# A two-layer encoder on one core: where a group's background steps stand, and GpSimd's block copies in program order

## The chip, the core and the metric

The kernel runs on one core of a Trainium2 chip. The core has five engines that each work through a queue of their own in order, and wait for each other by semaphores: TensorE (PE, matrix multiplies), VectorE (DVE), ScalarE (ACT), GpSimd (POOL) and SyncE (SP, whose queue issues all DMA transfers here). The metric is the device time of one execution in microseconds (us), as the median of several runs; beside it one execution was recorded by the hardware profiler, and all rows quoted below come from that.

## The reference, cut to what matters

Two layers on 256 tokens of width 2048, all in float32. Each layer first makes q, k and v for two attentions and two gates from one projection of the normalised input; q and k are normalised per head before they are used:

```python
h = rmsnorm(x, norm_mix[l]) * (1.0 + sc_a) + sh_a
qa, ka, va, qb, kb, vb, ga, gb = split_cols(h @ w_in[l])
qa = rotary_partial(rmsnorm(qa.reshape(B, S, HA, HEAD_DIM), qn_a[l]), pos)
ka = rotary_partial(rmsnorm(ka.reshape(B, S, GA, HEAD_DIM), kn_a[l]), pos)
ya = window_attention(qa, ka, va, sink_a[l]) @ w_proj_a[l]
qb = rmsnorm(qb.reshape(B, S, HB, HEAD_DIM), qn_b[l])
kb = rmsnorm(kb.reshape(B, S, HB, HEAD_DIM), kn_b[l])
yb = neighbourhood_attention(qb, kb, vb, rel_bias_b[l]) @ w_proj_b[l]
merged = jax.nn.sigmoid(ga) * ya + jax.nn.sigmoid(gb) * yb
x = x + gt_a * (merged @ w_out[l])
```

A gated feed-forward network with a convolution over three tokens follows. The first attention has 8 query heads on 2 key heads (window of 128 tokens to each side), the second 8 heads on a 4 x 64 grid with a bias table.

## The kernel before

**Weights and halves.** All weights pass through the core once, in units of 16 blocks of 128 x 128 (1 MB). A unit is one transfer into a `raw` buffer (4 of them, shared with the rows of `ada_w`). Each unit has two halves; ACT casts a half to a rounded value (L348), and DVE subtracts that from the original (L349), so that every matrix product is made of high and low parts and comes out near float32. A half is the tile `hl`, of which there are 4 buffers: ACT can cast a half as soon as PE is done with the one four places earlier. On PE a product of tokens is the lines L464 to L466, a product of features L391, L392 or L395 to L397.

**Groups.** The q, k and v columns come in nine groups of 512 columns (`QKV_GROUPS`), group 0 being k and v of the first attention, groups 1 and 2 its q, and 3 to 8 the parts of the second (4 and 7 are v). A group is four units, so eight halves. In layer 2 (`l == 1`) a group is one pass: `tokens` makes its products, and then `qk_rows` does the normalisation in these steps:

- the squares on ACT (L651, sums in `qss`), a scaling and addition on DVE (L534), and the power -1/2 on POOL (L535, written to `qrs`);
- `norm`, some ticks later: DVE multiplies the sums in PSUM by `qrs` (L661) into `qn`, a tile with one buffer (`bufs=1`), and applies the rotation (L678 to L680). In layer 2 L661 is kept in program order on DVE's queue;
- `turn`, a tick after that: the rows become columns. Either PE transposes them (L697) and ACT scales the result (L698), or, for the groups in `MOVED_QK` (0, 1, 2 and 8 of layer 2), DVE transposes blocks of 32 x 32 (L685), POOL carries the blocks to their places with 16 copies (`moved_blocks`, L320), and three ticks later ACT scales them (L689).

**Attention as background.** The heads are a generator (`attention`, heads 0 to 7 of the first attention and then those of the second). A step of a head has scores on PE (L727), a mask and maximum on DVE (L730), exponentials and a division on ACT (L739, L747). In layer 2 the probabilities are then turned the same way, DVE's block transposition (L326) into the place of the head's q and the one before it, and 16 copies on POOL (L320, named `p<-spare` for head 0 and `p<-packA` or `p<-packB` for the others). After these come a split (L481, L484), the product with v (L766) and another split (L769, L770). DVE's other background work is the product of rows of `ada_w` with the condition (L248, named `aw`).

**Ticks.** Whatever is background runs at a tick, which comes once a unit, at its last block: first the functions that were deferred to this tick (`bg.defer`, `later`), then as many steps of the attention as its rate allows (0.4 a tick at first in layer 2), then the transfers of `ada_w` that a plan prescribes. A group ends with a unit, so one tick falls on the end of each group, and before the change it ran inside `tokens`, ahead of the group's squares and power.

**Order.** The instructions are recorded in the order in which the program emits them; a scheduler then sets each engine's queue and may move an instruction ahead of others, save for those that are wrapped in `tc.keep_in_program_order`, which keep their place among each other and the rest of the program's order on that engine.

Of the kernel before, what the change touches and what calls it, by code (L numbers as in the profile page):

```python
# [139 lines left out]
UB = 16  # L140
# [5 lines left out]
def encoder(ctx: ExitStack, tc: tile.TileContext, a: dict, out: bass.AP):  # L146
    nc = tc.nc
# [159 lines left out]
    bg = Paced()  # L307

    def later(n, fn):

        if n == 0:
            fn()
        else:
            bg.defer(lambda: later(n - 1, fn))

    def moved_blocks(dst, src):

        for b in range(0, P, BLOCK):
            for a in range(0, P, BLOCK):
                nc.gpsimd.tensor_copy(  # L320
                    out=dst[a : a + BLOCK, :, :, b : b + BLOCK], in_=src[b : b + BLOCK, :, :, a : a + BLOCK]
                )

    def turned_blocks(src, rows, n):

# [47 lines left out]
    class Wide:  # L373
# [9 lines left out]
        def turned(self):  # L383

            return [half.rearrange("p r q -> p q r") for half in self.halves]
# [13 lines left out]
    class Stream:  # L399
# [51 lines left out]
                    sums = [turned_back(p) for p in sums]  # L451
                evac(ps[:, : S + 2] if isinstance(acts[0], tuple) else sums if wide else sums[0])

        def tokens(self, h, kcs):

            pss = [mm.tile([P, 512], F32, name=f"ps{self.l}_{self.u}_t{t}", tag="mm") for t in range(2)]
            for kc in kcs:
                for _ in range(4):
                    hl, j = self.next_block()
                j -= 3  # L460
                hi, lo = (turns(hl[:, i, j * P : (j + 4) * P]) for i in range(2))
                for t, ps in enumerate(pss):
                    xh, xl = (h[kc][:, i, t * P : (t + 1) * P] for i in range(2))
                    nc.tensor.matmul(ps[:], xh, hi, start=kc == kcs[0], stop=False)  # L464
                    nc.tensor.matmul(ps[:], xh, lo, start=False, stop=False)  # L465
                    nc.tensor.matmul(ps[:], xl, hi, start=False, stop=kc == kcs[-1])  # L466
                if self.l == 0 and self.u == 1 and self.at == 4:
                    warm(WARM_ROW)
                if self.at == UB:
                    self.tick()  # L470
            return [turned_back(ps[:]) for ps in pss]

# [171 lines left out]
    def qk_rows(pss, heads, rot, gain, dst, then, moved=False, pinned=False):  # L644

        n = heads * HEAD
        ss = sm.tile([P, 8], F32, name="qss", tag="qss")
        for t, ps in enumerate(pss):
            for i in range(heads):
                sq = at.tile([P, HEAD], F32, name="qsq", tag="qsq", bufs=1)  # L650
                nc.scalar.activation(  # L651
                    out=sq[:], in_=ps[:, i // 2, i % 2 * HEAD : i % 2 * HEAD + HEAD], func=AF.Square,
                    accum_out=ss[:, t * heads + i : t * heads + i + 1],
                )
        rs = sm.tile([P, 8], F32, name="qrs", tag="qrs")
        rsqrt(rs[:, : 2 * heads], ss[:, : 2 * heads], HEAD, 2 * heads)
        def norm():
            qn = at.tile([P, 8 * HEAD], F32, name="qn", tag="qn", bufs=1)[:, : 2 * n]
            qn = qn.rearrange("p (t h d) -> p t h d", t=2, d=HEAD)
            for t, ps in enumerate(pss):  # L660
                product = nc.vector.tensor_tensor(  # L661
                    out=qn[:, t].rearrange("p (a h) d -> p a h d", h=2),
                    in0=ps[:, : heads // 2].rearrange("p a (h d) -> p a h d", d=HEAD),
                    in1=rs[:, t * heads : (t + 1) * heads].rearrange("p (a h) -> p a h", h=2).unsqueeze(3).broadcast_to([P, heads // 2, 2, HEAD]),
                    op=ALU.mult,
                )
                if pinned:
                    tc.keep_in_program_order(product)
            if rot is not None:
                x1, x2 = qn[:, :, :, :HALF], qn[:, :, :, HALF:ROT]  # L670
                tab = [rot[:, i].unsqueeze(2).broadcast_to([P, 2, heads, HALF]) for i in range(4)]
                tm = []
                for i in range(2):
                    z = ev.tile([P, S], F32, name=f"rt{i}", tag="z")
                    z = z[:].rearrange("p (i t h d) -> p i t h d", i=2, t=2, h=4)
                    tm += [z[:, 0, :, :heads], z[:, 1, :, :heads]]
                for i, src in enumerate((x1, x2, x2, x1)):
                    nc.vector.tensor_tensor(out=tm[i], in0=src, in1=tab[i], op=ALU.mult)  # L678
                nc.vector.tensor_tensor(out=x1, in0=tm[0], in1=tm[1], op=ALU.subtract)
                nc.vector.tensor_tensor(out=x2, in0=tm[2], in1=tm[3], op=ALU.add)  # L680
            bg.defer(lambda: turn(qn))

        def turn(qn):
            if moved:
                nc.vector.transpose(out=qn, in_=qn)  # L685
                moved_blocks(dst.rearrange("p h (t s) -> p h t s", t=2), qn.rearrange("p t h d -> p h t d"))

                def scaled():
                    tc.keep_in_program_order(nc.scalar.activation(out=dst, in_=dst, func=AF.Identity, scale=gain))  # L689
                    then()  # L690

                later(QK_STEPS, scaled)
                return
            for t in range(2):
                ps = ax.tile([P, 4, P], F32, name="qtp", tag="ax")
                for h in range(heads):
                    nc.tensor.transpose(ps[:, h], qn[:, t, h], ident[:])  # L697
                scaled = nc.scalar.activation(  # L698
                    out=dst[:, :, t * P : (t + 1) * P], in_=ps[:, :heads], func=AF.Identity, scale=gain
                )  # L700
                if pinned:
                    tc.keep_in_program_order(scaled)
            then()

        bg.defer(lambda: bg.defer(lambda: bg.defer(norm)))

    def in_halves(src, name, tag, yes):

# [183 lines left out]
    for l in range(L):  # L892
        st = Stream(l) if l == 0 else nxt
# [116 lines left out]
        for pi, (groups, gates) in enumerate(parts):  # L1010
            last = pi == len(parts) - 1
            for g, part in enumerate(groups):
                have_h(part)
                pss = st.tokens(h, part)
                if pi == max(0, len(parts) - 2) and g == 0:
                    gains, sink, cw, rots = small(l)
                dst = packs[g // 3][:, 4 * (g % 3) : 4 * (g % 3) + 4]
                rows = dst.rearrange("p (t a) s -> p t a s", t=2)
                if not last or pi > 0:
                    for t, ps in enumerate(pss):  # L1020
                        if pi == 0:
                            nc.scalar.copy(rows[:, t], ps)
                        else:
                            nc.vector.tensor_tensor(out=rows[:, t], in0=ps, in1=rows[:, t], op=ALU.add)
                    pss = [rows[:, t] for t in range(2)]
                if not last:
                    continue

                def turned(g=g):
                    ready[0] = g + 1  # L1030

                vcol = {0: 1, 4: 0, 7: 0}.get(g)
                if vcol is not None and pi == 0:
                    for t in range(2):
                        nc.scalar.copy(rows[:, t, vcol:], pss[t][:, vcol:])
                if g == 0:
                    qk_rows(pss, GA, rots[1], gains[:, 1:2], kTa, turned, g in MOVED_QK[l], l == 1)
                elif g < 3:
                    qk_rows(pss, 4, rots[0], gains[:, 0:1], dst, turned, g in MOVED_QK[l], l == 1)
                elif vcol is None:  # L1040
                    qk_rows(pss, 4, None, gains[:, 3:4] if g in (3, 6) else gains[:, 2:3], dst, turned, g in MOVED_QK[l], l == 1)
                else:
                    turned()
                if g == (1 if l in EARLY else 2):
                    bg.add(job, ATT[l])


            have_h(gates)
            for mo in range(BARE[0] if l else 0, KC):

                def gate_a(ps):
                    src, to = ps, pair(ya[:, mo])
                    if pi > 0:
                        nc.vector.tensor_tensor(out=to, in0=ps, in1=to, op=ALU.add)
                        src = to
                    if last:
                        half_tanh(to, src)
                    elif pi == 0:
                        nc.scalar.copy(to, ps)

                st.features([hs[k] for k in gates], [gate_a])
# [234 lines left out]
```

## Time and profile before

| | us |
|---|---|
| median of 3 runs | 2586.07 |
| lowest and highest run | 2584.91 and 2586.75 |
| the profiled execution | 2584.3 |
| its span, first to last instruction | 2581.7 |
| TensorE busy | 2547.9 (99%) |
| VectorE busy | 2212.6 (86%) |
| ScalarE busy | 1454.8 (56%) |
| GpSimd busy | 263.1 (10%), nearly all of it between 1376 and 1711 us |

The profile has tables (busy time by engine, by group of instructions, by stretch of time) and rows in order of time. A row gives its start in us from the span's beginning, its duration, the engine, the line, the operation, the tiles written and read, and the shape; in square brackets, where the engine was idle before it, how long, and what released it. The groups 0 to 8 of layer 2 are multiplied from about 1352 to 1562 us, and the first attention's heads run from about 1446 to 1590 us.

### The profile page before, as it was taken

How to read it: one execution, taken by the hardware profiler on the slowest of the kernel's cores; microseconds unless marked ns; L12 is line 12 of the kernel's file. 1: busy time of each engine (PE TensorE's matmuls, PEld its weight loads, DVE VectorE, ACT ScalarE, POOL GpSimd, SP SyncE). 2: the span in 40 equal slices, each digit the busy share in tenths (PEclk: the TensorE clock that was granted, in tenths of full speed). 3: DMA queues.
4: the chain of work that ended last, by engine and by line, in shares of the span. 5: the costliest groups of instructions: out<-in, count | busy, mean ns of one | idle time of the engine just before them, and what ended most of it. 6: DMA issues, size and time to landing. Idle time of an engine off the chain costs nothing.

```text
span 2581.7 us, 43544 instructions
## 1 busy us (share of the span) xinstructions
PE 2547.9 (99%) x17324; PEld 2378.3 (92%) x17324; DVE 2212.6 (86%) x3227; ACT 1454.8 (56%) x2432; POOL 263.1 (10%) x345
## 2 busy tenths in 40 slices
PE   8999999999999999999999999999999999999999
PEld 7999899999999999999998879999999999999998
DVE  8998998998998899799987778879889987766775
ACT  5445765456663665466565566654576546644663
POOL 0001100000000000000003668730000000000000
PEclk9999999999999999999999999999999999999999
DMA  9998789986778778777767667778848775555554
GB/s 370 352 349 306 263 299 356 335 315 227 259 292 307 258 285 297 291 279 279 281 226 271 262 229 264 258 284 332 309 175 294 291 295 197 206 201 197 204 202 147
DMA packets 102158, 699.97 MB, mean 271 GB/s; under 512 B 12866, under 2 KB 15170, under 8 KB 18114
## 3 DMA queue, kind: packets, MB, share of 16 engines
q1 hardware_dynamic: 101954, 697.20, 73.0%
q8 instruction: 135, 2.21, 0.3%
q14 instruction: 69, 0.56, 0.1%
HBM read 695.06 MB, written 2.10 MB: 270 GB/s over the span
## 4 chain that ended last, share of the span: by engine, by line
PE 70%; DVE 14%; DMA 6%; ACT 4%; issue 4%; POOL 2%; SPq 0%; ACTq 0%; DVEq 0%; POOLq 0%
PE ps L391 31%; PE ps L392 15%; DVE hl L349 5%; PE ps L397 5%; PE ps L395 5%; PE ps L396 5%; DVE aw L248 4%; DMA aw<-in_aw 3%; PE ps_t L465 2%; PE ps_t L464 2%; PE ps_t L466 2%; ACT hl L348 2%; DMA w<-in_ws 2%; POOL p L320 1%; DVE x L1108 1%
## 5 line engine op out<-in xcount | busy, mean ns | idle before, releaser
L349 DVE TENSOR_TENSOR hl<-w,hl 128x1024 fp32r<-128x1024 f32 x928 | 1130.3, 1224 | 215.4 <-ACT hl L348 213.1
L348 ACT CAST hl<-w 128x1024 fp32r<-128x1024 f32 x928 | 964.7, 1046 | 587.0 <-PE ps L392 253.8
L391 PE MATMUL ps<-h,hl 128*128 128x512 f32 x2432 | 796.8, 382 | 0.0
L392 PE MATMUL ps<-h,hl 128*128 128x256 f32 x2432 | 662.9, 273 | 0.0
L391 PEld LDWEIGHTS ps<-h,hl 128*128 128x128 f32 x2432 | 459.7, 189 | 64.0
L392 PEld LDWEIGHTS ps<-h,hl 128*128 128x128 f32 x2432 | 466.9, 192 | 0.0
L248 DVE CUSTOM_DVE_ANT_0 aw<-aw,cact,ab 128x2048 f32<-128x2048 f32 x189 | 443.8, 2349 | 14.0 <-DMA aw<-in_aw 13.4
L395 PE MATMUL ps<-h,hl 128*128 128x256 f32 x896 | 247.3, 276 | 1.9 <-DVE ri L745 0.8
L397 PE MATMUL ps<-h,hl 128*128 128x256 f32 x896 | 245.9, 276 | 0.6 <-DVE hl L349 0.6
L396 PE MATMUL ps<-h,hl 128*128 128x256 f32 x896 | 246.4, 275 | 0.0
L465 PE MATMUL ps_t<-hl,h 128*128 128x512 f32 x576 | 220.4, 383 | 4.8 <-DVE hl L349 4.5
L464 PE MATMUL ps_t<-hl,h 128*128 128x512 f32 x576 | 217.7, 383 | 3.8 <-ACT h L571 2.4
L466 PE MATMUL ps_t<-hl,h 128*128 128x512 f32 x576 | 219.0, 381 | 0.0
L395 PEld LDWEIGHTS ps<-h,hl 128*128 128x128 f32 x896 | 171.9, 192 | 3.1 <-PE ps L397 0.9
L396 PEld LDWEIGHTS ps<-h,hl 128*128 128x128 f32 x896 | 172.0, 192 | 0.4 <-DVE h L572 0.2
L397 PEld LDWEIGHTS ps<-h,hl 128*128 128x128 f32 x896 | 171.6, 192 | 0.8 <-DVE hl L349 0.8
L391 PE MATMUL ps<-act_o,hl 128*128 128x512 f32 x512 | 170.5, 382 | 0.0
L1135 DVE SCALAR_TENSOR_TENSOR u<-both,cw,u 128x255 f32<-128x255 f32 x304 | 146.0, 480 | 3.8
L397 PE MATMUL ps<-merged,hl 128*128 128x256 f32 x512 | 140.8, 276 | 3.5 <-DVE hl L349 3.5
L395 PE MATMUL ps<-merged,hl 128*128 128x256 f32 x512 | 140.7, 275 | 0.4 <-ACT hl L348 0.4
L396 PE MATMUL ps<-merged,hl 128*128 128x256 f32 x512 | 140.6, 275 | 0.0
L392 PE MATMUL ps<-act_o,hl 128*128 128x256 f32 x512 | 139.6, 273 | 0.0
(242 smaller groups left out, 4867.6 us busy)
## 6 DMA issues: line engine op xcount, KB each, us to landing
w<-in_ws SPq DMA_DIRECT2D x463, 1024.0 KB, 4.9
aw<-in_aw SPq DMA_DIRECT2D x189, 1024.0 KB, 5.0
p<-in_bias SPq DMA_DIRECT2D x16, 256.0 KB, 4.9
x<-in_xT SPq DMA_DIRECT2D x4, 512.0 KB, 5.4
aw_o<-in_aw SPq DMA_DIRECT2D x2, 1024.0 KB, 12.8
out<-x SPq DMA_DIRECT2D x16, 128.0 KB, 2.2
w<-in_ws SPq DMA_DIRECT2D x2, 512.0 KB, 12.1
aw_b<-in_aw SPq DMA_DIRECT2D x1, 1024.0 KB, 17.9
```

What stands on the lines that cost most here:

```text
L248: product = nc.vector.tensor_tensor_reduce(out=raw[:], in0=raw[:], in1=cact[:], scale=1.0, scalar=ab[:, i : i + 1], op0=ALU.mult, op1=ALU. ...
L348: nc.scalar.copy(hl[:, 0], r)
L349: nc.vector.tensor_tensor(out=hl[:, 1], in0=r, in1=hl[:, 0].bitcast(F32), op=ALU.subtract)
L391: nc.tensor.matmul(ps[:], hi, act.both, start=first, stop=False)
L392: nc.tensor.matmul(ps[:, :S], lo, act.high, start=False, stop=last)
L395: nc.tensor.matmul(out, hi, act[0], start=first, stop=False)
L396: nc.tensor.matmul(ps[:, :S], hi, act[1], start=False, stop=False)
L397: nc.tensor.matmul(out, lo, act[0], start=False, stop=last)
L464: nc.tensor.matmul(ps[:], xh, hi, start=kc == kcs[0], stop=False)
L465: nc.tensor.matmul(ps[:], xh, lo, start=False, stop=False)
L466: nc.tensor.matmul(ps[:], xl, hi, start=False, stop=kc == kcs[-1])
L1135: nc.vector.scalar_tensor_tensor(out=u[:, to], in0=ps[:, of], scalar=w[:, j : j + 1], in1=u[:, to], op0=ALU.mult, op1=ALU.add)
```

## The change

In layer 2 the tick at the end of a group is held back inside `tokens` and is made after `qk_rows` has emitted the group's squares and power. The deferral of `norm` counts one tick more there, since the held tick now comes after it was deferred; it falls on the same unit as before. `turn`, the tick after, used to come with the last block of the next group, ahead of that group's squares and power, and now comes behind them. The 16 copies of `moved_blocks` are kept in program order on POOL.

```diff
@@ moved_blocks
-                nc.gpsimd.tensor_copy(
+                tc.keep_in_program_order(nc.gpsimd.tensor_copy(
                     out=dst[a : a + BLOCK, :, :, b : b + BLOCK], in_=src[b : b + BLOCK, :, :, a : a + BLOCK]
-                )
+                ))
@@ Stream
-        def tokens(self, h, kcs):
+        def tokens(self, h, kcs, held=False):
...
-                if self.at == UB:
+                if self.at == UB and not (held and kc == kcs[-1]):
                     self.tick()
@@ qk_rows
-        bg.defer(lambda: bg.defer(lambda: bg.defer(norm)))
+        later(4 if pinned else 3, norm)
@@ the loop over groups
-                pss = st.tokens(h, part)
+                pss = st.tokens(h, part, held=bool(l))
...
                     qk_rows(pss, 4, None, gains[:, 3:4] if g in (3, 6) else gains[:, 2:3], dst, turned, g in MOVED_QK[l], l == 1)
                 else:
                     turned()
+                if l:
+                    st.tick()
                 if g == (1 if l in EARLY else 2):
                     bg.add(job, ATT[l])
```

What this does to the queues can be read from the built programs. First POOL's queue in layer 2, from group 0's power on. `qrs` is a power, `packA_14134<-qn` the copies of groups 0 to 2, `p<-...` those of a head, `packB_1_14136<-qn` those of group 8. Before:

```order
L535 TENSOR_TENSOR qrs<-qss,mhalf 128x4
L320 COPY packA_14134<-qn 32x2x2x32 x16
L535 TENSOR_TENSOR qrs<-qss,mhalf 128x8
L320 COPY packA_14134<-qn 32x8x32 x16
L535 TENSOR_TENSOR qrs<-qss,mhalf 128x8
L320 COPY packA_14134<-qn 32x8x32 x16
L535 TENSOR_TENSOR qrs<-qss,mhalf 128x8
L320 COPY p<-spare_15076 32x4x32 x16
L320 COPY p<-packA_14134 32x4x32 x32
L535 TENSOR_TENSOR qrs<-qss,mhalf 128x8
L320 COPY p<-packA_14134 32x4x32 x16
L535 TENSOR_TENSOR qrs<-qss,mhalf 128x8
```

With the change:

```order
L535 TENSOR_TENSOR qrs<-qss,mhalf 128x4
L535 TENSOR_TENSOR qrs<-qss,mhalf 128x8
L320 COPY packA_14134<-qn 32x2x2x32 x16
L535 TENSOR_TENSOR qrs<-qss,mhalf 128x8
L320 COPY packA_14134<-qn 32x8x32 x16
L535 TENSOR_TENSOR qrs<-qss,mhalf 128x8
L320 COPY packA_14134<-qn 32x8x32 x16
L320 COPY p<-spare_15076 32x4x32 x16
L320 COPY p<-packA_14134 32x4x32 x16
L535 TENSOR_TENSOR qrs<-qss,mhalf 128x8
L320 COPY p<-packA_14134 32x4x32 x16
L535 TENSOR_TENSOR qrs<-qss,mhalf 128x8
```

Each of the powers of groups 1, 2, 3, 5 and 6 stands one block of 16 copies further ahead: those of groups 1 to 3 ahead of the copies of the group before, that of group 5 ahead of head 2's, that of group 6 ahead of head 3's. In the same way the power of group 8 stands ahead of the copies of head 6, as the end of the difference on POOL shows (three heads between the powers of groups 6 and 8 as before, and now two behind the latter):

```order
 L320 COPY p<-packA_14134 32x4x32 x48
 L535 TENSOR_TENSOR qrs<-qss,mhalf 128x8
-L320 COPY p<-packA_14134 32x4x32 x16
+L320 COPY p<-packA_14134 32x4x32 x32
 L320 COPY packB_1_14136<-qn 32x8x32 x16
```

The second place is ACT's queue at the end of group 6 (its sums are `ps_32_t`), where head 1's output `oA` and head 2's split `pT` stand. Before:

```order
L348 CAST hl_37_1_15613<-w_37_15608 128x1024
L698 ACTIVATE packB_0_14135<-qtp,gains_14273 128x4x128 x2
L769 CAST oA_0_14835<-po 128x256
L481 CAST pT<-p 128x512
L481 CAST qA_5_15551<-packA_14134 128x256
L651 ACTIVATE qsq,qss<-ps_32_t_15289 128x128 x2
L651 ACTIVATE qsq,qss<-ps_32_t_15290 128x128 x4
```

With the change:

```order
L348 CAST hl_37_1_15613<-w_37_15608 128x1024
L651 ACTIVATE qsq,qss<-ps_32_t_15289 128x128 x2
L651 ACTIVATE qsq,qss<-ps_32_t_15290 128x128
L769 CAST oA_0_14855<-po 128x256
L651 ACTIVATE qsq,qss<-ps_32_t_15290 128x128
L481 CAST pT<-p 128x512
L651 ACTIVATE qsq,qss<-ps_32_t_15290 128x128 x2
L698 ACTIVATE packB_0_14135<-qtp,gains_14273 128x4x128 x2
```

The scaling of group 5 (L698) and the two splits were ahead of six squares of group 6 and now stand among and behind them. On PE the six scores of head 4 move back by six matmuls with it, and in the built program they wait for DVE's part of that output split (L770) where they waited for L698. The built program also shows what the norms wait for: before, the norm of groups 1, 2 and 3 waits for its power; now it waits for the last copy of the group before, which reads the one buffer `qn`. SP's queue has the same order in both. In the first layer all queues are unchanged.

## The prediction

> **What bounds the kernel now.** I read the table of stretches first, then TensorE's (PE's) rows that began after a wait, then the rows of GpSimd (POOL), VectorE (DVE) and ScalarE (ACT) around those. The change touches the second layer's q, k and v stage and its attention, 1350 to 1720 us. The two stretches (us; busy time with instruction count of PE, weight loads, DVE, ACT, POOL; clock; DMA share; GB/s):
>
> ```profile
> 1350.00:1590.00 240.00, 233.48 (x1247) 207.78 (x1246) 183.17 (x261) 142.20 (x303) 144.22 (x196) 0.99 0.68 253
> 1590.00:1720.00 130.00, 129.43 (x1159) 129.24 (x1159) 109.91 (x170) 77.28 (x141) 94.81 (x132) 1.00 0.73 270
> ```
>
> PE is the bound. Between 1350 and 1590 it idles 6.5 us, so only what opens or closes PE's gaps counts. These are the gaps (start, duration, instruction, last the wait ahead of it), with one of the first layer to compare:
>
> ```profile
> 274.70 0.33 PE L758 MATMUL tp<-ident,p 128*128 128x128 f32 x1 [2.37 <-ACT p L747]
> 1435.69 0.48 PE L465 MATMUL ps_t<-hl,h 128*128 128x512 f32 x1 [0.65 <-DVE hl L349]
> 1452.49 0.48 PE L465 MATMUL ps_t<-hl,h 128*128 128x512 f32 x1 [0.33 <-DVE hl L349]
> 1500.95 0.48 PE L465 MATMUL ps_t<-hl,h 128*128 128x512 f32 x1 [2.78 <-DVE hl L349]
> 1512.25 1.65 PE L727 MATMUL sc<-kA,qA 128*128 128x256 f32 x6 [2.62 <-ACT packB L698]
> ```
>
> A gap can cost more than its length. The column behind POOL's is the granted clock:
>
> ```profile
> 275.00:276.00 1.00, 1.00 (x9) 0.87 (x7) 1.00 (x2) 0.22 (x2) 0.00 (x0) 1.00 0.45 164
> 1502.00:1504.00 2.00, 2.00 (x6) 1.57 (x5) 2.00 (x7) 0.00 (x0) 0.00 (x0) 0.50 0.40 66
> 1504.00:1506.00 2.00, 2.00 (x8) 1.61 (x8) 2.00 (x5) 1.38 (x6) 0.00 (x0) 0.70 0.99 418
> 1512.00:1514.00 2.00, 1.75 (x7) 1.75 (x8) 1.70 (x3) 1.62 (x5) 1.88 (x4) 0.50 1.01 352
> 1514.00:1516.00 2.00, 2.00 (x7) 1.58 (x7) 1.68 (x7) 1.87 (x10) 1.79 (x6) 0.64 0.73 270
> ```
>
> After 2.78 and 2.62 the clock is halved for over 3 us, which loses 2x0.50 + 2x0.30 = 1.6 and 2x0.50 + 2x0.36 = 1.7. After 2.37 it stays at 1.00: the line lies between 2.37 and 2.62. The four gaps and two slow stretches make 6.4 + 3.3 = 9.7 us, the most that any edit here can win. [...]
>
> **Why the gaps are there.** POOL runs the power (L535) and the block copies (L320) in one queue:
>
> ```profile
> 1384.40 11.88 POOL L320 COPY packA<-qn 32x128 f32<-32x128 f32 x16 [5.37 <-DVE qn L685]
> 1397.16 1.64 POOL L535 TENSOR_TENSOR qrs<-qss,mhalf 128x8 f32<-128x8 f32 x1 [0.88 <-DVE qss L534]
> 1410.21 13.58 POOL L320 COPY packA<-qn 32x256 f32<-32x256 f32 x16 [11.42 <-DVE qn L685]
> 1423.87 1.64 POOL L535 TENSOR_TENSOR qrs<-qss,mhalf 128x8 f32<-128x8 f32 x1
> 1430.85 17.42 POOL L320 COPY packA<-qn 32x256 f32<-32x256 f32 x16 [5.35 <-DVE qn L685]
> 1448.35 1.64 POOL L535 TENSOR_TENSOR qrs<-qss,mhalf 128x8 f32<-128x8 f32 x1
> 1486.75 9.97 POOL L320 COPY p<-packA 32x128 f32<-32x128 f32 x16 [0.81 <-DVE packA L326]
> 1496.81 1.64 POOL L535 TENSOR_TENSOR qrs<-qss,mhalf 128x8 f32<-128x8 f32 x1
> ```
>
> Three of these powers stand right behind copies, and DVE's next norm (L661, pinned in its queue ahead of the weight halves that PE needs) waits for them:
>
> ```profile
> 1400.83 2.35 DVE L248 CUSTOM_DVE_ANT_0 aw<-aw,cact,ab 128x2048 f32<-128x2048 f32 x1
> 1403.10 1.28 DVE L661 TENSOR_TENSOR qn<-ps_t,qrs 128x512 f32<-128x512 f32 x2
> 1415.23 1.41 DVE L349 TENSOR_TENSOR hl<-w,hl 128x1024 fp32r<-128x1024 f32 x1 [1.23 <-ACT hl L348]
> 1418.97 0.35 DVE L534 TENSOR_SCALAR qss<-qss 128x8 f32<-128x8 f32 x1
> 1425.54 1.29 DVE L661 TENSOR_TENSOR qn<-ps_t,qrs 128x512 f32<-128x512 f32 x2 [3.76 <-POOL qrs L535]
> 1443.01 0.35 DVE L534 TENSOR_SCALAR qss<-qss 128x8 f32<-128x8 f32 x1
> 1450.02 1.29 DVE L661 TENSOR_TENSOR qn<-ps_t,qrs 128x512 f32<-128x512 f32 x2 [4.20 <-POOL qrs L535]
> 1490.03 0.25 DVE L534 TENSOR_SCALAR qss<-qss 128x8 f32<-128x8 f32 x1
> 1498.48 1.29 DVE L661 TENSOR_TENSOR qn<-ps_t,qrs 128x512 f32<-128x512 f32 x2 [5.85 <-POOL qrs L535]
> ```
>
> **Part 1: groups 0 to 3. The power goes first, but the wait stays and grows.** The norm of group g+1 writes the one buffer `qn` (bufs=1) that the copies of group g read, so it waits for those copies whatever POOL's order. The change puts them behind the power of g+1, which waits for that group's squares. The scaling of group g on ACT (L689) waits for the same copies, ahead of the casts. How long the copies then last follows from single ones in the chain of waits and the next norm's row above:
>
> ```profile
> 1415.60 1.29 POOL packA L320
> 1416.93 2.36 POOL packA L320
> 1422.52 0.40 POOL packA L320
> 1422.95 0.40 POOL packA L320
> 1491.59 1.19 POOL p L320
> ```
>
> Under a DVE instruction a copy takes as long as that instruction (1.29, 2.36); while DVE stands at its norm (after 1422) they follow each other in 0.43. A small copy (32x128) then takes 0.33: of the 16 that start at 1486.75, four, the last at 1491.59, fill the time up to DVE's idle 5.85, and the other twelve end at 1496.7, within 3.9. A DVE blocked by the copies speeds them up, which is what I build on.
>
> Group 0: the power ends at 1397.16 + 1.64 = 1398.8. Up to 1403.1, with DVE mostly busy, about five copies pass; the other eleven take 3.6. The norm of group 1 starts at 1406.9, 3.8 late. Group 2's L534 then comes at 1418.97 + 3.8, less some 1.7 of idle that DVE makes up in between (1.23 of it in the row at 1415.23): about 1421.1, its power ends at 1423.0, one copy passes under the subtraction behind it, fifteen take 6.5: norm 2 at 1430.1, 4.6 late. Likewise L534 of group 3 at 1443.01 + 4.6, less 1.1 made up (an estimate: DVE idles less here) = 1446.5, power to 1448.5, copies to 1455.5: norm 3 starts 5.5 late. PE resumed 2.47 after that norm (1452.49 against 1450.02) and will again: **+5.5**. On PE this shows as four gaps of 1.2 to 2.0 in place of 0.65 and 0.33, all under the clock's line. Bounds: with all sixteen copies at 0.33 and all idle of DVE caught up, +3; with the lengths that the rows above show for whole groups (11.88, 13.58, 17.42) the norms come 7.6, 14 and 25 late: +25. I take +5.5, since the 0.40 rows are of exactly this state, POOL copying while DVE stands at a norm.
>
> **Part 2: groups 5 and 6, heads 2 to 4.** Here the copies are an attention head's, on which the norm does not depend. The power of group 5 goes ahead of those of head 2: it can run at 1490.3, just behind L534, and is done when DVE reaches the norm at 1492.6. The 5.85 vanish, and with them the gap of 2.78 and its slow stretch: 4.4. The second gap stays in another form: the six scores of head 4 stand six matmuls later and wait for the subtraction L770, whose ACT half now stands behind five squares of group 6:
>
> ```profile
> 1514.64 0.28 ACT L651 ACTIVATE qsq<-ps_t 128x128 f32<-128x128 f32 x1
> ```
>
> At 0.3 to 0.4 each, after two casts of 1.05, L770 ends about 1508.4, while PE is there at 1506.5 (1512.25 - 2.62 - 4.4, and six matmuls, some 1.3): a gap of about 2.0 for 2.62, probably with no slow stretch: 0.6 + 1.7 more. One thing comes back: head 3's copies now stand behind group 6's power (about 1510 to 1511.7), and head 4's transposition (L326) overwrites what they read. Sixteen small copies, about half of them under DVE instructions, take 6: DVE stands until about 1517.7, goes on with the product (2.35 in the row at 1400.83), the norm and a subtraction, and PE loses about 1.2 before the half that needs it. Sum 4.4 + 2.3 - 1.2 = **-5.5**. Bounds: -6.7 if that last wait is hidden, -2.5 if the scores wait 4 us and the clock halves.
>
> **Part 3: group 8 and head 7.** The same exchange once more:
>
> ```profile
> 1553.93 9.53 POOL L320 COPY p<-packA 32x128 f32<-32x128 f32 x16 [0.81 <-DVE packA L326]
> 1564.74 3.61 POOL L535 TENSOR_TENSOR qrs<-qss,mhalf 128x8 f32<-128x8 f32 x1 [1.28 <-DVE qss L534]
> 1569.25 0.71 DVE L326 STREAM_TRANSPOSE packA<-p 128x512 f32<-128x512 f32 x1
> 1578.73 1.30 DVE L349 TENSOR_TENSOR hl<-w,hl 128x1024 fp32r<-128x1024 f32 x1
> 1586.33 1.05 ACT L348 CAST hl<-w 128x1024 fp32r<-128x1024 f32 x1 [0.47 <-PE ps L397]
> ```
>
> Before, POOL was idle ahead of this power; nobody waited long. Now head 6's copies start behind it at 1568.3 and, mostly with DVE at a stand, end near 1574.4. Head 7's L326 moves there from 1569.25, 5.1 late, and so does the half at 1578.73, done at 1585.2. PE ended that half at 1586.3 (the cast at 1586.33 waits for it). A half is 24 matmuls here, and 130 us held 1159, so it took 2.7 and was begun at 1583.6: a gap of 1.6. The copies of head 7 and group 8 follow 5 us late, at most 2 more through L689. **+2**, between 0 and +4.5.
>
> No matmul, DMA or copy is added or removed, layer 1 has the same order, and DVE's and ACT's other exchanges are of instructions of under 1.3 us inside the same tick. Sum 5.5 - 5.5 + 2 = **+2.0**. The profiled execution is 2584.3 us (span 2581.7); the runs shown have a median of 2586.07, so the forecast is 2586.3 for such a profile and **2588.1** on the median.
>
> **Rivals.** A difference within 0.2% (5.2 us) is about what a measurement can't tell from none.
> - *Slower: the copies don't hurry.* The rows for it are the whole groups (0.74 to 1.09 per copy); against it stands 0.40 in the blocked state. Each 0.1 us per copy costs 16 x 0.1 in each of three groups, 4.8 in all, so a mean 0.07 above mine decides. With a mean of 0.6 it is 2.0 + 8 = +10: 2596; at full length +22: 2608. Chance 0.27.
> - *Faster: part 1 is hidden.* The weight halves lie ready a few deep ahead of PE. If that lead and DVE's idle time swallow all but 2 us of part 1 and all of part 3, the sum is 2 - 5.5 = -3.5: 2582.5, and at the other bounds -6: 2580. Against it: norm 3 already holds up PE in the rows at 1450 to 1452. Chance 0.15.
> - *The change doesn't do its work at head 4.* The scores wait for L770 well over 2.6 us, the clock halves again, and part 2 gives -2.5: +5, 2591. For it: ACT is the fullest just there. Chance 0.15, half of it within 0.2%.
>
> **Numbers.** Forecast 0.43: within +-4 of 2588.1. Faster by over 0.2%: 0.09 (0.07 of the second rival, 0.02 of the forecast's edge); slower by over 0.2%: 0.32 (0.25 of the first, 0.07 of the third); no difference: 0.59. The range 2582 to 2598 leaves out the first rival's far end and the second's.
>
> **What will show it.** Right: the powers at about 1397, 1421, 1447 and 1490, each with no copies ahead; norms of groups 1 to 3 late by 4 to 6 us, waiting for L320 and no longer for L535; no wait at group 5's norm; four PE gaps under 2.4 us before 1460 and no halved clock. Wrong: block copies of groups 0 to 2 that last over 10 us after their power (first rival); PE without gaps before 1460 (second); a halved clock near 1510 (third).

## The result and the profile after

| | us |
|---|---|
| before, median of 10 runs | 2586.66 |
| changed, median of 10 runs | 2594.19 (2591.10 to 2598.05) |
| ratio | 1.0024, 95% interval 1.0015 to 1.0033 |
| the changed kernel's profiled execution | 2596.36, span 2594.6 |

The ratio, which compares the means of the runs, is worth 6.2 us, from 3.9 to 8.5; the two medians are 7.5 us apart. The kernel became slower. The time lies in the range of the prediction, but 6 us above the forecast of 2588.1, and on a side that had been given 0.32.

The spans of the two profiles differ by 12.9 us, and 7.0 of these have nothing to do with the change: the changed kernel is 7.03 us late already at 1340 us, in the first layer, whose order is the same. A second profile of the changed kernel (below) is 1.3 late there, and the profiles of the experiments, whose first layer is the same too, lie between 0.2 and 7.0. Lateness here means: the start of one matmul in a trace, less the start of the same matmul in the trace of before (counted by line in the queue's order). It is the measure used in all that follows, with its value at 1340 taken off. By stage, in the trace of before's times:

| | 1340 to 1495 (part 1) | to 1575 (part 2) | to 1715 (part 3) | sum |
|---|---|---|---|---|
| predicted | +5.5 | -5.5 | +2 | +2.0 |
| changed, first profile | +7.7 | -7.7 | +6.0 | +5.9 |
| changed, second profile | +6.6 | -6.6 | +5.5 | +5.4 |

The two stretches of the changed kernel that answer to those shown of before, with 7 us added to the times (busy time and count of PE, weight loads, DVE, ACT and POOL, clock, DMA share, GB/s). PE idles 8.4 us in the first, where it was 6.5, and 4.5 in the second, where it was 0.6:

```profile
1357.00:1597.00 240.00, 231.64 (x1239) 205.44 (x1237) 179.06 (x259) 139.06 (x300) 121.95 (x190) 0.99 0.67 250
1597.00:1727.00 130.00, 125.50 (x1115) 124.55 (x1114) 110.18 (x169) 75.58 (x140) 98.05 (x137) 1.00 0.71 266
```

PE's rows behind a wait, in the changed kernel:

```profile
1417.49 0.48 PE L465 MATMUL ps_t<-hl,h 128*128 128x512 f32 x1 [0.78 <-DVE hl L349]
1440.19 0.48 PE L465 MATMUL ps_t<-hl,h 128*128 128x512 f32 x1 [1.72 <-DVE hl L349]
1447.41 0.48 PE L465 MATMUL ps_t<-hl,h 128*128 128x512 f32 x1 [1.68 <-DVE hl L349]
1465.94 0.61 PE L465 MATMUL ps_t<-hl,h 128*128 128x512 f32 x1 [2.04 <-DVE hl L349]
1521.84 0.38 PE L727 MATMUL sc<-kA,qA 128*128 128x256 f32 x1 [1.15 <-DVE oA L770]
1591.54 0.38 PE L397 MATMUL ps<-h,hl 128*128 128x256 f32 x1 [0.72 <-DVE hl L349]
1622.68 0.38 PE L397 MATMUL ps<-oA,hl 128*128 128x256 f32 x1 [1.40 <-DVE hl L349]
1684.13 0.38 PE L397 MATMUL ps<-h,hl 128*128 128x256 f32 x1 [1.56 <-DVE hl L349]
1714.61 0.38 PE L397 MATMUL ps<-h,hl 128*128 128x256 f32 x1 [1.40 <-DVE hl L349]
```

The first four are part 1, as predicted in number; predicted were 1.2 to 2.0 each, and the first is shorter (0.78, with one of 0.27 just ahead of it). The 2.78 at group 5's half is gone, the scores' gap is 1.15 in place of 2.62 and no clock is halved there: part 2. The last four are part 3; only the first of them had been foreseen (1.6). POOL's queue of the changed kernel from group 1's power to group 2's copies:

```profile
1404.19 1.64 POOL L535 TENSOR_TENSOR qrs<-qss,mhalf 128x8 f32<-128x8 f32 x1 [18.13 <-DVE qss L534]
1405.78 8.26 POOL L320 COPY packA<-qn 32x128 f32<-32x128 f32 x16
1428.29 2.48 POOL L535 TENSOR_TENSOR qrs<-qss,mhalf 128x8 f32<-128x8 f32 x1 [14.25 <-DVE qss L534]
1430.72 6.97 POOL L320 COPY packA<-qn 32x256 f32<-32x256 f32 x16
1454.04 2.48 POOL L535 TENSOR_TENSOR qrs<-qss,mhalf 128x8 f32<-128x8 f32 x1 [16.36 <-DVE qss L534]
1456.47 6.96 POOL L320 COPY packA<-qn 32x256 f32<-32x256 f32 x16
```

The copies do hurry: 16 in 6.97 us (0.44 each), where before they took 13.58 and 17.42. POOL waits 14 to 18 us for each power's squares with the copies of the group before standing behind it. And these are the rows that wait for the copies, of DVE (norms, and head 7's transposition) and of ACT (scalings of groups 1 and 8):

```profile
1414.07 0.69 DVE L661 TENSOR_TENSOR qn<-ps_t,qrs 128x512 f32<-128x512 f32 x1 [3.82 <-POOL packA L320]
1437.72 0.69 DVE L661 TENSOR_TENSOR qn<-ps_t,qrs 128x512 f32<-128x512 f32 x1 [7.31 <-POOL packA L320]
1437.72 1.15 ACT L689 ACTIVATE packA<-packA,gains 128x1024 f32<-128x1024 f32 x1 [5.26 <-POOL packA L320]
1463.46 0.69 DVE L661 TENSOR_TENSOR qn<-ps_t,qrs 128x512 f32<-128x512 f32 x1 [7.30 <-POOL packA L320]
1580.68 0.71 DVE L326 STREAM_TRANSPOSE packA<-p 128x512 f32<-128x512 f32 x1 [4.50 <-POOL p L320]
1606.48 1.15 ACT L689 ACTIVATE packB<-packB,gains 128x1024 f32<-128x1024 f32 x1 [5.50 <-POOL packB L320]
```

At 1437.72 DVE and ACT are released at the same moment, by the same last copy. Behind PE's gap of 2.04 us at 1465.94 the clock is halved, from 1466.2 to 1469.6; the table of stretches of the changed kernel shows 0.54 and 0.60 there:

```profile
1466.00:1468.00 2.00, 2.00 (x5) 1.60 (x6) 2.00 (x7) 1.99 (x4) 0.00 (x0) 0.54 0.00 0
1468.00:1470.00 2.00, 2.00 (x7) 1.63 (x6) 1.15 (x4) 2.00 (x6) 0.00 (x0) 0.60 0.29 57
```

### The profile page after: what moved, and what is told of

It is laid out like the page before. It is cut to its first block, busy times and chain, and to the rows that moved or that the text cites. A ratio compares the mean times of both kernels' runs of the same rounds, so it can differ in the third digit from the quotient of the medians.

```text
span 2594.6 us, 43545 instructions
## 1 busy us (share of the span) xinstructions
PE 2553.8 (98%) x17324; PEld 2382.8 (92%) x17324; DVE 2212.7 (85%) x3227; ACT 1454.7 (56%) x2432; POOL 243.9 (9%) x345
```

## The experiments

All kernels compute the whole reference. In the four kernels with another place for the norm or for head 7 the code has one line more, and the scaling is line L690 there. The table gives each kernel's stages as above and its ratio to before; a halved clock costs 1.7 us where it falls into the stage (an estimate: the halved stretches of the two traces of before and of the changed kernel last 3.41 us at 0.50), and its time is given.

| kernel | part 1 | part 2 | part 3 | sum | halved at | ratio (95%) |
|---|---|---|---|---|---|---|
| changed | +7.7 | -7.7 | +6.0 | +5.9 | 1466 | 1.0024 (1.0015 to 1.0033) |
| changed again | +6.6 | -6.6 | +5.5 | +5.4 | none | 1.0025 (1.0015 to 1.0035) |
| copies in order, no tick held | -0.2 | -6.8 | -0.8 | -7.7 | none | 0.9975 (0.9965 to 0.9985) |
| the same again | +0.1 | -5.0 | -0.4 | -5.4 | 1509 | 0.9981 (0.9969 to 0.9992) |
| held at 5 and 6 | 0.0 | -4.9 | -0.6 | -5.6 | 1517 | 0.9985 (0.9976 to 0.9994) |
| held at 0 to 3 | +7.8 | -8.0 | -0.7 | -0.9 | 1461 | 1.0007 (0.9996 to 1.0018) |
| held at 8 | -0.2 | -5.1 | +5.45 | +0.2 | 1514 | 0.9996 (0.9987 to 1.0005) |
| all held, copies free | +0.1 | -1.4 | -0.6 | -1.9 | 1507, two stretches | 1.0000 (0.9991 to 1.0009) |
| 0 to 3, other place for the norm | +7.9 | -5.0 | 0.0 | +2.9 | 1440, 1519 | 1.0015 (1.0006 to 1.0024) |
| the same, scaling later | +1.45 | -4.9 | +0.8 | -2.7 | 1514 | 0.9984 (0.9973 to 0.9996) |
| 8, scaling later | +0.2 | -6.7 | +3.9 | -2.7 | none | 0.9996 (0.9987 to 1.0006) |
| 8, other place for head 7 | -0.2 | -6.8 | +5.8 | -1.1 | none | 0.9997 (0.9987 to 1.0007) |
| 8, both | -0.1 | -6.7 | +4.2 | -2.7 | none | 0.9998 (0.9989 to 1.0006) |

### Which part costs what: the tick held at some groups only

The first four kernels ran together. In each the copies keep program order; the groups at which the tick is held differ:

```diff
-                pss = st.tokens(h, part, held=bool(l))
+                now_held = bool(l) and g in (5, 6)
+                pss = st.tokens(h, part, held=now_held)
...
-                if l:
+                if now_held:
                     st.tick()
```

(with the norm's deferral of 4 ticks where the tick is held and 3 where not), and in the second and third kernel `(0, 1, 2, 3)` and `(8,)`.

> The tick is held only at groups 5 and 6, the copies keep program order: part 2 alone. Theory A (the three parts are independent, and each has its own cause in its own swap): between the middle of group 0 and the end of the attention the trace loses nothing before 1480 us and gains 7.7 us by 1560 us (as the changed kernel does there), and keeps it: about 2579 us, ratio 0.997. Theory B (the loss behind 1580 us is the transfers' lead, spent by any shift of work in the stage): the gain of 7.7 is given back behind 1580 us by 3 us or more, 2582 us or later.

> The tick is held only at groups 0 to 3, the copies keep program order (which by itself puts group 5's power ahead of head 2's copies). Theory A: the norms of groups 1 to 3 wait 3.8, 7.3 and 7.3 us for block copies, PE has gaps of about 1 to 2 us there, the trace loses 6 us by 1460 (7.7 if the clock is halved once), gains some 4.6 back at group 5, and loses nothing behind 1580: about 2588 us. Theory B: behind 1580 us it loses 3 us or more too, since the lead is spent by part 1: 2591 us or later.

> The tick is held only at group 8, the copies keep program order. Theory A: no loss before 1460, about 4.6 us gained at group 5 (its power goes ahead), and the whole loss of 6 us behind 1580: head 7's block transposition waits about 4.5 us for copies, ACT's scaling of group 8 about 5.5 us: about 2588 us. Theory B: a loss behind 1580 of under 2 us, since nothing was lost before: 2583 us.

The fourth holds no tick, so that of the whole change only this is left:

```diff
-                nc.gpsimd.tensor_copy(
+                tc.keep_in_program_order(nc.gpsimd.tensor_copy(
```

> No tick is held; only the block copies keep program order. POOL's queue then differs from before in two places: group 5's power stands ahead of head 2's copies, and head 1's behind as they were. Theory A: group 5's norm waits no more, the gap of 2.78 us and its halved clock go (4.5 us), the gap at head 4's scores stays in some form between 1 and 3 us: 2582 us, from 2580 to 2584. Rival: the scores of head 4 wait for the same ACT scaling at the same time as before, so that what is won at the first gap is given back at the second: 2586 us.

The medians are 2581.16, 2587.54, 2585.59 and 2578.55 us: the first misses its 2579 (part 2 gains 5.0 there and not 7.7, with one halved clock), the third is below its 2588, and the last is below its range. The parts are independent (theory A): part 1's loss is there when only groups 0 to 3 are held, and nothing is lost behind 1580 then; part 3's is there when only group 8 is. Theory B is refuted: -0.7 and -0.6 behind 1575 in the kernels without group 8.

The surprise is the fourth. It has the instructions of PE, DVE, ACT and SP in before's order, and POOL's but for one exchange: group 5's power stands ahead of head 2's 16 copies, where the program has it; the scheduler had put it behind. This alone is worth the whole of part 2, and it is the fastest kernel of all: 2578.55 us (11 runs), 0.25% under before, and 0.19% in the second measurement. Its rows at the place (POOL, DVE and PE, and ACT's scaling of group 8):

```profile
1491.29 2.47 POOL L535 TENSOR_TENSOR qrs<-qss,mhalf 128x8 f32<-128x8 f32 x1 [4.35 <-DVE qss L534]
1493.72 11.77 POOL L320 COPY p<-packA 32x128 f32<-32x128 f32 x16
1493.80 0.69 DVE L661 TENSOR_TENSOR qn<-ps_t,qrs 128x512 f32<-128x512 f32 x1 [0.39 <-POOL qrs L535]
1508.02 0.38 PE L727 MATMUL sc<-kA,qA 128*128 128x256 f32 x1 [2.12 <-ACT packB L698]
1587.19 1.16 ACT L689 ACTIVATE packB<-packB,gains 128x1024 f32<-128x1024 f32 x1 [1.22 <-POOL packB L320]
```

The norm's wait is 0.39 in place of 5.85, and head 2's copies, which now stand behind the power, are waited for by nobody for long. The scores' gap stays at 2.12, and in this execution without a halved clock; its second measurement (2.15 and a halved clock at 1509) keeps 1.8 us less in part 2 (-5.0 against -6.8). Holding the tick at groups 5 and 6 adds nothing to this: its -4.9 with one halved clock against -6.8 with none and -5.0 with one.

### The queue on POOL or the steps on the other engines

All ticks held as in the change, but the copies left to the scheduler. It then puts POOL's queue back as it was before, word for word, while some 15 instructions of ACT, DVE and PE stay moved.

```diff
-                tc.keep_in_program_order(nc.gpsimd.tensor_copy(
+                nc.gpsimd.tensor_copy(
```

> All ticks held as in the changed kernel, but the copies are left to the scheduler: GpSimd's queue is then the one of before, word for word, while ScalarE and VectorE keep most of what the held ticks moved. Theory A (the order on GpSimd makes the whole difference): within 1.5 us of before, the gap of 2.8 at group 5's half is there with its halved clock: 2586 us. Rival (the held ticks cost by what they move on ScalarE and VectorE): 2 us or more slower: 2589 us.

Its median is 2586.94 us, its ratio 1.0000. Theory A holds: neither part 1 nor part 3 shows (+0.1, -0.6). PE's two rows of part 2:

```profile
1507.50 0.80 PE L465 MATMUL ps_t<-hl,h 128*128 128x512 f32 x1 [2.83 <-DVE hl L349]
1520.00 0.38 PE L727 MATMUL sc<-kA,qA 128*128 128x256 f32 x1 [1.41 <-DVE oA L770]
```

The gap at group 5's half is as before, and the scores' is 1.41 in place of 2.62. So the six matmuls by which the held tick moves the scores do win about 1.2 us, as part 2 had it, but only while the gap ahead of them stays; with that gone, PE comes earlier and waits longer again (2.27 in the second profile of the change; 1.15 in the first, where PE comes 1.1 us later).

### Part 1: which wait

Two things wait for the late copies: the norm on DVE, since it overwrites `qn`, and the scaling L689 on ACT. First the norm's wait was taken away, by another place for groups 1 and 3, the argument `other` (the tick held at groups 0 to 3):

```diff
-            qn = at.tile([P, 8 * HEAD], F32, name="qn", tag="qn", bufs=1)[:, : 2 * n]
+            whole = at.tile([P, 8 * HEAD], F32, name="qn", tag="qn", bufs=1) if other is None else other
+            qn = whole[:, : 2 * n]
...
+    packs[2][:, 4 * (g // 2) : 4 * (g // 2) + 4].rearrange("p a s -> p (a s)") if l and g in (1, 3) else None
```

> As the kernel with the tick held at groups 0 to 3, but the norms of groups 1 and 3 write into the place of the parts of groups 6 and 7 (free until then) instead of qn, so that they no longer wait for the copies of groups 0 and 2, nor group 2's norm for those of group 1. Theory A (the norm's wait for the copies is the loss of part 1): L661 waits under 1 us, the copies slow down to 12 us and more per group since VectorE works on beside them, and by 1476 us the trace has lost under 2 us where it lost 8.1 (1.7 of it a halved clock): about 2581 us. Rival (ScalarE's scaling L689, ahead of the casts, waits for the same copies): with slow copies it waits longer, and 4 us or more stay lost: 2585 us or later.

The norms wait no more, and nothing is won: +7.9 (two halved clocks fall into the stage and the one behind), 2590.39 us. What waits now (ACT's scaling of group 2, and DVE's split of a q behind it; POOL's copies):

```profile
1452.59 8.02 POOL L320 COPY packA<-qn 32x256 f32<-32x256 f32 x16
1460.64 1.15 ACT L690 ACTIVATE packA<-packA,gains 128x1024 f32<-128x1024 f32 x1 [8.52 <-POOL packA L320]
1463.07 0.43 DVE L484 TENSOR_TENSOR qA<-packA,qA 128x256 fp32r<-128x256 f32 x1 [7.17 <-ACT qA L481]
```

The rival holds: ACT stands 8.52 us ahead of its casts, and DVE stands behind ACT. The copies did not slow down much (8.02 us for 16, against 6.96 in the changed kernel): DVE still stands, for 7.17 us in the row above. Then the scaling was deferred by a tick as well:

```diff
-                later(QK_STEPS, scaled)
+                later(QK_STEPS + extra, scaled)
```

with `extra` 1 for groups 0 to 2 of layer 2.

> As the kernel in which the norms of groups 1 and 3 write elsewhere (no wait of L661 for copies), and the scaling L689 of groups 0, 1 and 2 is deferred by one tick more. Theory A (late copies cost only through these two waits, one on VectorE, one on ScalarE, and either alone is enough): with both gone the trace loses under 2 us by 1476 against before, and with group 5's gain it ends at about 2580 us. Rival (the next one down the line takes the wait, the split of group 1's q or the first heads): 4 us or more stay lost by 1490, 2585 us.

Now part 1 costs +1.45 (theory A, under 2), with the scaling of group 2 still waiting 6.1 us; ratio 0.9984. So the scaling's wait alone keeps the whole loss (+7.9, with a halved clock, as +7.8 with both waits), and with both waits dealt with the loss all but goes. That the norm's wait alone would be enough too was not tried.

### Part 3: which wait

The same was done for group 8: first the scaling two ticks later (`extra` 2 for group 8), which moves L689 and no other instruction.

> As the kernel with the tick held at group 8, but the scaling L689 of group 8 is deferred by two ticks more; on every engine but ScalarE the order is the same. Theory A (ScalarE stands 5.5 us at L689 ahead of casts): that wait goes, the PE gaps of 1.48, 1.38 and 0.90 us behind 1610 go, about 0.7 stays at 1585: 4.5 us of the 5.5 come back, 2581 us. Rival B (head 7's transposition and everything behind it on VectorE and GpSimd is 6 us late): at least 3 us stay lost behind 1580, 2585 us.

Then, without that, another place for head 7's transposed probabilities, so that it doesn't wait for head 6's copies; no instruction moves:

```diff
-                return qTa[:, i - 1 : i + 1] if i else paired(F32, f"spare{l}")
+                return qTa[:, (3 if i == 7 else i - 1) : (5 if i == 7 else i + 1)] if i else paired(F32, f"spare{l}")
```

> As the kernel with the tick held at group 8, but head 7's transposed probabilities L326 go to the place of heads 3 and 4, whose copies have long been done, instead of that of 6 and 7: same order on every engine, the 4.5 us wait for head 6's copies is gone. Theory A (VectorE's stand at L326 and ScalarE's at L689 each make a part): the PE gap of 0.7 us at 1585 goes, the later ones, which come from L689, stay: 1 to 2 us less than with the wait, about 2584 us. Rival B (VectorE's stand was the only cause): 4 us less, 2581 us. A third way: VectorE busy again slows the copies (1.2 to 2.4 us each in place of 0.43), L689 waits even longer, and nothing is won: 2586 us.

And both:

> Both at once with the tick held at group 8: head 7's other place, and the scaling L689 of group 8 two ticks later. Theory A: both stands are gone, and of the 5.5 us behind 1580 under 1.5 stay: about 2580 us, as with the copies' order alone. Rival (GpSimd's copies themselves come too late for the heads of the second attention): 3 us or more stay, 2583 us or later.

With no part of this the loss behind 1575 is 6.2 us (+5.45 against -0.8 with the copies' order alone). The later scaling leaves 4.7, head 7's place 6.6, both 4.9. Theory A fails in all three: taking out the waits that the profile names brings back a quarter at most, and the ratios show not even that (0.9996 to 0.9998, as with neither). With head 7's place alone DVE works on, and the copies are slow again (0.64 us each for the heads and 0.78 for group 8, by the rows that follow); these are POOL's rows (heads 6 and 7 in one, then group 8) and ACT's:

```profile
1561.68 20.59 POOL L320 COPY p<-packA 32x128 f32<-32x128 f32 x32
1582.33 12.44 POOL L320 COPY packB<-qn 32x256 f32<-32x256 f32 x16
1594.81 1.16 ACT L690 ACTIVATE packB<-packB,gains 128x1024 f32<-128x1024 f32 x1 [7.18 <-POOL packB L320]
```

That is the third way of the expectation: the scaling waits 7.18 in place of 5.5. With both mended the next one down the line takes the wait, the split of head 8's probabilities on ACT, as the rival of the last expectation had it:

```profile
1581.58 15.39 POOL L320 COPY packB<-qn 32x256 f32<-32x256 f32 x16
1597.02 17.07 POOL L320 COPY p<-packB 32x128 f32<-32x128 f32 x32
1603.21 0.62 ACT L481 CAST pT<-p 128x512 fp32r<-128x512 f32 x1 [4.79 <-POOL p L320]
```

From the power of group 8 on POOL has no pause of a microsecond until head 9's copies are through: head 6, head 7, group 8, heads 8 and 9, 80 copies in over 50 us (1572.77 to 1626.7 in the changed kernel, with pauses of 0.81 and 0.58). Head 6's copies begin some 12 us later than before, and within this row moving one reader only shows the next. Behind it the copies hold up little. The chain of waits that ends at PE's gap of 1714.61 in the changed kernel passes, from 1608.57 on, through no copy, but through the steps of the second attention's heads on DVE and ACT and through four transfers of a head's bias table:

```profile
1633.82 5.67 DMA p<-in_bias
1647.38 5.87 DMA p<-in_bias
1666.79 5.46 DMA p<-in_bias
1696.95 6.63 DMA p<-in_bias
```

Before, the chain that ends at the gap of 0.57 at 1701.66 already ran through two such transfers (5.68 us at 1653.77 and 6.53 at 1684.12). So the late copies seem to hand their delay to heads that had little time to spare. This is read from the chains and not tested, and how the 4.9 us that remain divide among the later heads was not tried.

### The change and the copies' order side by side

> The changed kernel once more, beside the next one on the same chip. If the 7 us by which its first profile was behind ahead of 1350 us are chance of that execution (two halved clocks and a slower start in the first layer, whose order is the same), this profile is within 3 us of before there, and loses again 5.5 to 6.5 us between 1350 and 1720: about 2592.5 us, ratio 1.0024. If the change itself slows the first layer, the 7 us are there again.

> The copies' program order alone, once more beside the changed kernel: ratio to before 0.9965 to 0.9985 as in its first runs, about 2580 us, some 12 us less than the changed kernel. If its first result was a lucky share of halved clocks, it lies within 3 us of before.

On one chip the changed kernel took 2594.31 us and the copies' order alone 2581.22, about as expected of both. The 7 us ahead of 1350 were chance: the second profile is 1.3 late there. Its gap at group 3's norm and the one at the scores, both without a halved clock behind them this time:

```profile
1460.33 0.48 PE L465 MATMUL ps_t<-hl,h 128*128 128x512 f32 x1 [2.17 <-DVE hl L349]
1516.12 0.38 PE L727 MATMUL sc<-kA,qA 128*128 128x256 f32 x1 [2.27 <-DVE oA L770]
```

## Why the prediction was right, and where it was wrong

The time lay in the range (2582 to 2598), the sign of the sum was right, and its size was not: +2.0 against +6.2 (3.9 to 8.5) by the ratio, +5.9 and +5.4 by the traces. "No difference" had the largest chance, 0.59, and the kernel is slower by more than the 0.2% that was named, if only just (the interval reaches down to 0.15%). The narrower band, within 4 us of 2588.1, was missed. The range held the time by luck: its upper part was there for the first rival, whose mechanism did not occur.

**Part 1, the mechanism: right, shown in the profile after.** The wait of L661 moved from the power to the copies. With the 7.03 of the first layer taken off, norms 1 to 3 start at 1407.0, 1430.7 and 1456.4; predicted were 1406.9, 1430.1 and 1455.5. The copies took 0.44 us each behind the power, against 0.43 from the chain of waits. The size: +5.5 predicted, +6.6 without a halved clock, +7.7 with one. The gaps themselves come to 0.27 + 0.78 + 1.72 + 1.68 + 2.04 = 6.5, less the 1.0 of before 5.5; what was missing is some 1.1 us beside them (a gap's first row lasts 0.48 in place of 0.38, and the matmuls around it start late), and the halved clock behind the gap of 2.04 (3.41 us at 0.50). The working named the norm as the wait and mentioned L689 beside it; the runs showed that L689 alone keeps the whole loss.

**Part 2: right in sum, wrong in its reason.** -5.5 predicted, -6.6 and -7.7 measured. The loss that was to come back at head 4 (1.2) is hidden: L326 waits 3.2 us there, and no half comes late. The other difference is the attribution: the 2.3 at the scores were put down to the six matmuls and the split's place, that is, to the held tick. The copies' order alone wins as much.

**Part 3 is the step that failed.** "The copies of head 7 and group 8 follow 5 us late, at most 2 more through L689. +2, between 0 and +4.5." It measured +6.0 and +5.5, above its own bound. The gap that the working followed, at head 7's half, was 0.72 and not 1.6; the three behind it (1.40, 1.56, and 1.40 for 0.57), with some 1.5 us in smaller delays, make the rest. The reckoning stopped at the first reader of late copies, on a queue that then runs without a pause for over 50 us, and put the readers behind it (L689, then the second attention's heads) at 2 us at most; with the wait of that first reader taken out, 6.6 us were still lost.

**The rivals.** "The copies don't hurry" fell: 6.97 us per group. Its time, 2596 and later, is near the measured one only because part 3 cost what part 1 did not. "Part 1 is hidden" fell with four gaps. "The change doesn't do its work at head 4" fell too: no halved clock near 1510, and part 2 gave more than forecast, not less. None of the rivals had group 8 as its place.

**The clock's line.** The prediction drew it between gaps of 2.37 and 2.62 us. The traces have no such line by a gap's length: the clock was halved behind the gap of 2.04 in part 1 of the first profile, where the signs named no halved clock, and stayed at 1.00 behind the 2.17 at the same place in the second profile and behind 3.04 in another kernel (last section).

## What to carry to other kernels

A queue that serves a short urgent instruction and blocks of slow work can be put in order the wrong way round in both directions: ahead of a block whose readers come soon, the urgent one makes the whole block late, and every later reader with it. So before swapping, ask for each pair which of the two has the earlier reader; here one swap of six was right (group 5's power ahead of head 2's copies, which are read late) and won 0.19 to 0.25%, the one at group 6 changed nothing, and those at groups 1 to 3 and at 8 together lost more than the first had won. Follow the delayed block beyond the first instruction that waits for it: to the point where its queue has a pause, and along the steps of its last reader.

## What the runs showed of the hardware

**Where PE's clock was halved.** In the traces of before and of the changed kernel each halved stretch ahead of the last matmuls lasted 3.41 us, and within one trace they start whole multiples of 3.413 us apart: at 1501.8 and 1512.0 us before (3 times 3.413), and at 274.9, 551.4, 1466.2 and 1807.5 us in the changed kernel (81, 268 and 100 times). Counted off in such stretches from the halved ones, the two traces have five between 20 us and the last matmuls in which PE idles 2.0 us or more, and behind each of them the clock was halved: 2.59 and 2.38 us before, 2.23, 2.15 and 2.04 in the changed kernel. Of the three with 1.71 to 1.73 us one was followed by a halved stretch (1.71, ahead of 1807.5), of the five with 1.50 to 1.67 none. What decides between these was not tested.

So behind gaps of nearly the same length the clock was halved in one trace, which makes 1.7 us (3.41 us at 0.50), and not in another. The gap near 275 us lasts 2.37 us before, 0.64 of it in one such stretch and 1.73 in the next, and the clock stays at 1.00. In the changed kernel it lasts 2.40, of which 2.23 lie in one, and the clock behind it is 0.50:

```profile
275.09 0.48 PE L758 MATMUL tp<-ident,p 128*128 128x128 f32 x1 [2.40 <-ACT p L747]
275.00:278.00 3.00, 2.91 (x9) 2.45 (x10) 2.35 (x4) 1.32 (x5) 0.00 (x0) 0.50 0.90 319
```

A pair at one place of the program, later in the second layer: a gap of 2.47 us, all of it in one stretch, and the clock is 0.50 in the next (head 7's other place alone; PE's row, and the two stretches),

```profile
1870.44 0.41 PE L397 MATMUL ps<-merged,hl 128*128 128x256 f32 x1 [2.47 <-DVE hl L349]
```

```profile
1867.25:1870.67 3.42, 0.95 (x9) 0.76 (x8) 3.42 (x6) 0.00 (x0) 0.00 (x0) 1.00 0.39 89
1870.67:1874.08 3.41, 3.41 (x18) 3.41 (x18) 3.41 (x7) 1.94 (x4) 0.00 (x0) 0.50 1.01 425
```

and one of 3.04, in the kernel with both mended: 1.39 us of it lie in the first and 1.65 in the second of the stretches shown, PE idles 1.31 in the third, and the clock stays at 1.00:

```profile
1868.28 0.38 PE L397 MATMUL ps<-merged,hl 128*128 128x256 f32 x1 [3.04 <-DVE hl L349]
```

```profile
1863.22:1866.63 3.41, 2.02 (x19) 1.82 (x17) 2.63 (x4) 0.25 (x1) 0.00 (x0) 1.00 0.21 89
1866.63:1870.04 3.41, 1.76 (x15) 1.76 (x16) 3.41 (x7) 0.19 (x1) 0.00 (x0) 1.00 0.70 243
1870.04:1873.46 3.42, 2.10 (x16) 1.73 (x15) 3.42 (x7) 2.80 (x6) 0.00 (x0) 1.00 0.98 362
```

(behind a stretch stand its length and PE's busy time; the clock is the third number from the end). Single executions of one kernel here spread over 7 to 13 us, and one such halving more or less is 1.7 of it, by the estimate from 3.41 us at 0.50: two kernels are to be compared by many runs, or in the traces with the halved stretches counted.
